# The first stage of a two-layer decoder step: queue order, the place of the first weights, and the loads of the tap rows

## The chip, the cores and the metric

One Trainium2 chip, one core of it, one launch. The number is the device time of one execution in microseconds (us), lower is better. TensorE, VectorE, ScalarE, GpSimd and SyncE are called PE, DVE, ACT, POOL and SP, as in the profile; "PEld" is PE's load of the stationary operand.

## The reference, cut to what matters

A prompt of 512 tokens and a sample of 8 sequences with 4 tokens each go through two layers of width 1024 in fp32. The part that this change touches is the beginning of layer 0:

```
m = silu(c) @ ada_w[0, 0] + ada_b[0, 0]          # c: 1 + 8 rows; shift, scale, gate
h = x * (1 + scale) + shift                      # the modulation
a, g = split(h @ conv_pw1_w + conv_pw1_b)        # 1024 -> 2048
u = a * sigmoid(g)
y = depthwise convolution of u over 31 tokens, then a norm, silu and a product with conv_pw2_w
```

After it come a residual and norm, an MLP of width 4096, layer 1 with stick-breaking attention over a paged cache of 2048 tokens for each sample, and a second MLP.

## The kernel before, in words

The prompt lies transposed in SBUF, eight tiles of 128 features by 512 tokens. A product in near-fp32 is made of three fp32r matmuls (`mm3`, lines 310 to 315: high weight by high x, low by high, high by low), so each weight tile is split by ACT (the rounded copy, `wsplit`, line 304) and DVE (the rest, line 305), and each h tile likewise (lines 329 and 330). The Tile framework writes all semaphores and, with a simulated timeline, the order of each engine's instructions; a `NoSync` edge (`order`, line 317) or `tc.issue_after` fixes the order of two instructions on one engine. An instruction's place in an engine's queue is thus not its place in the text, but each engine runs its queue in order.

The first stage in the text:

- c, constants and the first four blocks of `ada_w` (`ada_load`, line 189, 1 MB each, two transfers, SP's queue) are loaded; the second four follow when the ring of four buffers has room. The parameter rows `prow` go over ACT's queue (lines 201 to 208), x over POOL's (line 216).
- x is transposed by PE into PSUM and copied back by DVE (lines 586 to 595).
- The modulation is made in two halves `h` of 512 columns of shift and of scale: four blocks each with products into one PSUM tile (line 606), a copy by ACT (line 609), a turn to feature-major (`to_fm`, line 548), and the bias (lines 636 to 638). Half 0 gives h tiles 0 to 3, half 1 tiles 4 to 7 (lines 640 and 641).
- Four chunks c of `conv_pw1_w` (loop at line 738) are staged by `wstage` on ACT's queue, two loads of 1 MB for a chunk, three buffers. Each chunk serves the sample (line 747) and the prompt. Chunk 0 holds four weight tiles split ahead and runs k outermost over four PSUM accumulators:

```
            for k in range(KT):
                for a, (whi, wlo) in zip(accs, ws):
                    mm3(a, whi[:, k, :], wlo[:, k, :], hhi[k], hlo[k], k == 0, k == KT - 1)
```

- `axd` (lines 647 to 650) is x times a constant, spilled to DRAM by POOL's queue for the residual much later. `ud` holds the prompt's u in DRAM with zero padding, written at lines 629 and 630, from which the convolution is read again (line 683).
- Two feature tiles of the convolution are done by DVE with 30 steps each (line 670), the other six by PE (line 693).
- The attention's head biases are loaded by 20 small DMAs on POOL's queue (lines 818 and 824), with the page table and a broadcast of the biases (828, 830).

From there two generators, one for the sample and one for the prompt, are merged by written costs into one stream.

Of the kernel before, what the change touches and what calls it, by code (L numbers as in the profile page):

```python
# [8 lines left out]
F32 = mybir.dt.float32  # L9
# [10 lines left out]
KT = 8  # L20
# [48 lines left out]
C1_W = 128 + 32 + 64 + 32  # L69
# [3 lines left out]
def shape_consts():  # L73
# [11 lines left out]
    c1 = np.concatenate([ident, sel4, sel2, nmask, causal], 1)  # L85
# [25 lines left out]
def yoco_step_kernel(  # L111
# [64 lines left out]
    nmask = c1[:, 224:256]  # L176
    ones32 = base.tile([P, 32], F32, name="ones32")
# [10 lines left out]

    def ada_load(n):
        blk = ring("adaw")  # L190
        h, kk = divmod(n, 4)
        for kp in range(2):
            r = kk * 256 + kp * P
            dma(blk.rearrange("p (k o c) -> p k o c", k=2, o=2)[:, kp],
                ada_w[0, 0, r : r + P, 0 : 2 * D].rearrange("p (o f) -> p o f", o=2)[:, :, h * 512 : h * 512 + 512])
        first_blk.append(blk)
# [11 lines left out]
    nc.scalar.dma_start(prow[25:56, 0:D], conv_dw_w[0])  # L208
# [86 lines left out]
    def wstage(src, k):  # L295
        st = wp.tile([P, 2048], F32, tag="stage", bufs=STB, name="stage")
        nc.scalar.dma_start(st.rearrange("p (k c) -> p k c", k=k), src.rearrange("(k p) c -> p k c", p=P))
        return st.rearrange("p (k c) -> p k c", k=k)

    def wsplit(st, c0, cw, wp=wp):  # L300
# [3 lines left out]
        nc.scalar.copy(hi, st[:, :, c0 : c0 + cw])  # L304
        vec.tensor_tensor(lo, st[:, :, c0 : c0 + cw], hi.bitcast(F32), op=ALU.subtract)  # L305
        return hi, lo
# [280 lines left out]
    for hf in range(2):  # L587
        pts = []
        for kk in range(4):
            pts.append((pm if kk < 3 else aux)("xT"))  # L590
            for i in range(4):
                tr(pts[kk][:, i * P : i * P + P], xn[2 * i + hf][:, kk * P : kk * P + P], ident)
        for kk in range(4):
            ubuf[4 * hf + kk] = xn[2 * kk + hf]
            vec.tensor_copy(xn[2 * kk + hf], pts[kk])
    a00 = base.tile([P, KT, 9], F32, name="a00")
    b00 = base.tile([P, KT, 9], F32, name="b00")
    ada_sb = []
    for h in range(2):
        acc = aux("ada_A00")  # L600
        for kk in range(4):
            if h:
                ada_load(4 + kk)
            blk = first_blk[4 * h + kk]
            for g in range(4):
                mm(acc[32 * g : 32 * g + 32, :], cT[:, 2 * kk + g // 2, :], blk[:, g * 512 : g * 512 + 512],
                   start=(kk == 0), stop=(kk == 3), tile_position=(0, 32 * g))
        sb = stmp([P, 512], "ada0", tag="s512")
        last_act = nc.scalar.copy(sb, acc)
        ada_sb.append(sb)  # L610

    pt = aux("pt_p")
    for k in range(KT):
        tr(pt[:, k * 64 : k * 64 + NR], prow[0:NR, k * P : k * P + P], ident[0:NR, 0:NR])
    vec.tensor_copy(prm.rearrange("p r k -> p k r"), pt.rearrange("p (k r) -> p k r", k=KT)[:, :, 0:NR])
    vec.tensor_scalar_mul(aln, prm[:, R_LNG : R_LNG + 8, :], ALPHA)

    spt = aux("xsT")
    for k in range(KT):
        tr(spt[:, k * 32 : k * 32 + 32], xs_row[:, k * P : k * P + P], ident[0:32, 0:32])  # L620
    xsT = sfm("xsT", "sv", 2)
    vec.tensor_copy(xsT, spt[:, 0:256].rearrange("p (k t) -> p k t", k=KT))
# [4 lines left out]
    vec.memset(utail, 0.0)  # L627
    ud = dr.tile([KT, P, T + 32], F32, name="ud")
    pdma(ud[:, :, 0 : CW - 1].rearrange("k p t -> p k t"), utail[:, :, 0 : CW - 1])
    pdma(ud[:, :, T + CW - 1 :].rearrange("k p t -> p k t"), utail[:, :, 0:2])  # L630
    hhi, hlo = xtiles()
    for k in range(KT):
        if k % 4 == 0:
            us = to_fm(ada_sb[k // 4], "adat_A00")
            for t, o in ((b00, 0), (a00, 1)):
                vec.tensor_tensor(t[:, k : k + 4, :], us[:, 4 * o : 4 * o + 4, 0:9],
                                  prm[:, o, k : k + 4].unsqueeze(2).to_broadcast([P, 4, 9]), op=ALU.add)
            vec.tensor_scalar_add(a00[:, k : k + 4, :], a00[:, k : k + 4, :], 1.0)
        h = tmp("h")
        act(h, ubuf[k], AF.Identity, scale=a00[:, k, 8:9], bias=b00[:, k, 8:9])  # L640
        split(h, hhi[k], hlo[k])
    s_h = sfm("hT0", "hT", 2)
    vec.tensor_tensor(s4(s_h), s4(xsT), smod(a00), op=ALU.mult)
    vec.tensor_tensor(s4(s_h), s4(s_h), smod(b00), op=ALU.add)
    s_ax = sfm("sax", "sax")
    vec.tensor_scalar_mul(s_ax, xsT, ALPHA)
    for k in range(KT):
        t = tmp("ax0")
        nc.scalar.mul(t, ubuf[k], ALPHA)
        pdma(axd[0][k], t)  # L650

# [86 lines left out]
    for c in range(4):  # L738
        with tc.issue_after((first_act if c == 0 else last_act).ins):
            st = [wstage(conv_pw1_w[0, :, o * D + c * 256 : o * D + c * 256 + 256], KT) for o in range(2)]  # L740
# [16 lines left out]
        for i in range(2):  # L757
# [5 lines left out]
            vec.tensor_copy(sfull[:, kt, :, CW - 1 : CW + 3], su[:, kt, :].rearrange("p (s q) -> p s q", q=NQ))  # L763
        accs = []
        if c == 1:
            state_in()
            sconv(0)
        if c:
            sconv(c)
        if c == 0:  # L770
            p1c = ExitStack()
            plc = pool(p1c, "p1c", "right")
            ws = [wsplit(st[o], i * P, P, plc if i else wp) for i in range(2) for o in range(2)]
            accs = [pm("pw1") for _ in range(3)] + [aux("pw1")]
            for k in range(KT):
                for a, (whi, wlo) in zip(accs, ws):
                    mm3(a, whi[:, k, :], wlo[:, k, :], hhi[k], hlo[k], k == 0, k == KT - 1)
            p1c.close()
# [8 lines left out]
        for i in range(2):  # L787
# [21 lines left out]
            if kt not in TAPS:  # L809
                pdma(ud[kt][:, CW - 1 : T + CW - 1], u)  # L810
# [4 lines left out]

    bq = base.tile([P, 8], F32, name="bq")
    for g in range(4):
        pdma(bq[32 * g : 32 * g + 32, 0:4],
            attn_bias[0].rearrange("(q g) -> g q", g=4)[g : g + 1, :].to_broadcast([32, 4]))
        for hh in range(2):  # L820
            r = 32 * g + 16 * hh
            for u in range(2):
                hd = u * 8 + hh * 4 + g
                pdma(bq[r : r + 16, 4 + u : 5 + u], attn_bias[0:1, hd : hd + 1].to_broadcast([16, 1]))
    nbq = base.tile([P, 2], F32, name="nbq")
    nc.gpsimd.tensor_scalar_mul(nbq, bq[:, 4:6], -1.0)
    ptab = base.tile([P, NS, NPG], I32, name="ptab")
    pdma(ptab.rearrange("p s g -> p (s g)"), page_table.rearrange("(o s) g -> o (s g)", o=1).to_broadcast([P, NS * NPG]))
    bias_p = base.tile([P, 2 * H], F32, name="bias_p")
    pdma(bias_p[:, 0:H], attn_bias.to_broadcast([P, H]))  # L830
    nc.gpsimd.tensor_scalar_mul(bias_p[:, H:], bias_p[:, 0:H], -1.0)
# [640 lines left out]
```

## Time and profile before

| | us |
|---|---|
| median of 3 runs (lowest to highest) | 1671.01 (1669.94 to 1671.44) |
| the profiled execution | 1672.76 |
| its span, first to last instruction | 1671.0 |
| PE busy in it | 1564.6 (94%) |
| DVE busy | 956.5 (57%) |
| ACT busy | 568.6 (34%) |
| POOL busy | 188.4 (11%) |

The busy share is a mean over stages. Whether a shorter first stage makes the whole shorter depends on what the first stage waits for and on whether the engines behind it are full or wait for something that does not move with it.

### The profile page before, as it was taken

The page shows a single profiled execution, that of the slowest core. Times are in us where ns is not written, and L with a number is a line of the kernel's source. Part 1 is how long each engine was busy: PE and PEld are TensorE (multiplying, and loading weights), DVE is VectorE, ACT ScalarE, POOL GpSimd, SP SyncE. Part 2 cuts the span into 40 slices and gives each one's busy share as a digit, 9 for nine tenths or more (in the row PEclk, how much of TensorE's full clock was granted, in tenths as well). Part 3 has the DMA queues.
Part 4 walks back from the last instruction along what each step waited for, and adds up shares of the span by engine and source line. Part 5 has one row for each costly group of instructions (what it writes and reads, how often), then busy time and mean ns, then how long its engine had stood idle before and what let it go on. Part 6 is the DMA issues. An engine that isn't in the chain of part 4 may idle for free.

```text
span 1671.0 us, 25460 instructions
## 1 busy us (share of the span) xinstructions
PE 1564.6 (94%) x10489; PEld 1090.3 (65%) x10489; DVE 956.5 (57%) x1812; ACT 568.6 (34%) x903; POOL 188.4 (11%) x221
## 2 busy tenths in 40 slices
PE   4899988989999999999899999889889999999995
PEld 2566424656777777777468775546777767556885
DVE  2399637385576755655643457975774533332546
ACT  1322105153332332323332444852272323223332
POOL 4100110000112111110012112021101000000002
PEclk9899999989999999999999999999999999999998
DMA  8787879878676866576879878355546585995221
GB/s 292 247 294 265 265 230 393 318 261 309 235 267 243 322 227 234 218 279 227 318 271 316 296 239 325 134 213 185 192 162 244 184 312 180 356 346 191 85 70 51
DMA packets 152968, 409.25 MB, mean 245 GB/s; under 512 B 8807, under 2 KB 82823, under 8 KB 128261
## 3 DMA queue, kind: packets, MB, share of 16 engines
q1 hardware_dynamic: 48739, 159.76, 25.7%
q0 software_dynamic: 23584, 149.07, 24.7%
q10 hardware_dynamic: 80530, 98.80, 17.8%
q8 instruction: 82, 1.34, 0.3%
q14 instruction: 33, 0.27, 0.0%
HBM read 390.57 MB, written 17.88 MB: 244 GB/s over the span
## 4 chain that ended last, share of the span: by engine, by line
PE 73%; issue 10%; DVE 8%; DMA 6%; ACT 1%; POOL 1%; SPq 0%; DVEq 0%; ACTq 0%; POOLq 0%
PE pd L311 17%; PE pd L315 17%; PE pd L314 17%; PE zt L1001 3%; PE av L1052 3%; PE sd_acc L535 2%; PE cv L693 2%; DMA stage<-in_conv_pw_w_dram 2%; PE w_acc L562 1%; DVE v L670 1%; PE ada_A L237 1%; PE lnT L350 1%; DMA kraw<-in_cache_k_dram,krow 1%; PE pw L311 1%; PE pw L314 1%
## 5 line engine op out<-in xcount | busy, mean ns | idle before, releaser
L305 DVE TENSOR_TENSOR wlo<-stage,whi 128x1024 fp32r<-128x1024 f32 x184 | 223.3, 1217 | 252.2 <-ACT whi L304 251.8
L304 ACT CAST whi<-stage 128x1024 fp32r<-128x1024 f32 x184 | 191.6, 1046 | 423.1 <-PE pd L315 353.1
L311 PE MATMUL pd<-xhi,whi 128*128 128x512 f32 (+1 forms) x832 | 321.0, 387 | 11.3 <-ACT whi L304 5.5
L314 PE MATMUL pd<-xhi,wlo 128*128 128x512 f32 (+1 forms) x832 | 318.9, 384 | 2.1 <-DVE wlo L305 2.0
L315 PE MATMUL pd<-xlo,whi 128*128 128x512 f32 (+1 forms) x832 | 313.0, 387 | 5.5 <-DVE xlo L444 5.0
L995 DVE STREAM_TRANSPOSE kt<-kraw 128x512 f32<-128x512 f32 x256 | 164.3, 685 | 123.7 <-DMA kraw<-in_cache_k_dram,krow 84.0
L311 PE MATMUL pd<-h2h,whi 128*128 128x512 f32 (+1 forms) x544 | 206.7, 388 | 1.6 <-DVE v L1170 1.0
L315 PE MATMUL pd<-h2l,whi 128*128 128x512 f32 (+1 forms) x544 | 205.2, 383 | 0.0
L314 PE MATMUL pd<-h2h,wlo 128*128 128x512 f32 (+1 forms) x544 | 204.9, 381 | 0.0
L311 PEld LDWEIGHTS pd<-xhi,whi 128*128 128x128 f32 x832 | 161.1, 194 | 60.9 <-issue 14.3
L315 PEld LDWEIGHTS pd<-xlo,whi 128*128 128x128 f32 x832 | 157.0, 193 | 58.4 <-issue 15.4
L314 PEld LDWEIGHTS pd<-xhi,wlo 128*128 128x128 f32 x832 | 161.0, 193 | 42.8 <-issue 12.7
L1170 DVE SCALAR_TENSOR_TENSOR v<-pd,mod_B,v 128x512 f32<-128x512 f32 x120 | 87.8, 745 | 115.8 <-PE pd L315 115.4
L973 POOL DMA_INDIRECT kraw<-in_cache_k_dram,krow x64 | 65.9, 1029 | 631.1 <-DVE kt L995 396.0
L311 PEld LDWEIGHTS pd<-h2h,whi 128*128 128x128 f32 x544 | 101.9, 188 | 34.6 <-issue 10.4
L1145 ACT ACTIVATE relu<-pd 128x512 f32<-128x512 f32 (+1 forms) x68 | 38.9, 572 | 240.3 <-PE pd L315 235.1
L315 PEld LDWEIGHTS pd<-h2l,whi 128*128 128x128 f32 x544 | 101.8, 188 | 28.6 <-issue 9.4
L314 PEld LDWEIGHTS pd<-h2h,wlo 128*128 128x128 f32 x544 | 102.2, 188 | 25.2 <-issue 6.7
L973 POOL DMA_INDIRECT vt<-in_cache_v_dram,vrow x64 | 67.0, 1047 | 273.7 <-PE av L1052 235.3
L1001 PE MATMUL zt<-kt,qb 128*32 128x128 f32 x2048 | 77.0, 280 | 5.2 <-DVE kt L995 5.2
L1001 PEld LDWEIGHTS zt<-kt,qb 128*32 128x32 f32 x2048 | 53.4, 111 | 30.3 <-issue 14.7
L352 DVE BATCH_NORM_STATS2 bn<-lnT 128x6 f32<-128x128 f32 x160 | 36.5, 285 | 62.4 <-PE lnT L350 62.2
(299 smaller groups left out, 2014.6 us busy)
## 6 DMA issues: line engine op xcount, KB each, us to landing
sw<-in_mlp_w_dram SPq DMA_DIRECT2D x64, 1024.0 KB
stage<-in_mlp_w_dram ACTq DMA_DIRECT2D x64, 1024.0 KB
adaw<-in_ada_w_dram SPq DMA_DIRECT2D x40, 1024.0 KB
stage<-in_conv_pw_w_dram ACTq DMA_DIRECT2D x12, 1024.0 KB
adaw<-in_ada_w_dram SPq DMA_DIRECT2D x16, 512.0 KB
swkv<-in_w_kv_dram SPq DMA_DIRECT2D x8, 1024.0 KB
stage<-in_w_kv_dram ACTq DMA_DIRECT2D x8, 1024.0 KB
ur<-ud POOLq DMA_DIRECT2D x24, 270.0 KB, 7.5
```

Of the source, the lines that this page charges most:

```text
L304: nc.scalar.copy(hi, st[:, :, c0 : c0 + cw])
L305: vec.tensor_tensor(lo, st[:, :, c0 : c0 + cw], hi.bitcast(F32), op=ALU.subtract)
L311: first = mm(out, whi, xh, start=start, stop=False)
L314: mm(out, wlo, xh, start=False, stop=False)
L315: latest[:] = [mm(out, whi, xl, start=False, stop=stop)]
L352: vec.bn_stats(self.st[:, i, k, :], pt[:, i * P : i * P + P])
L973: nc.gpsimd.indirect_dma_start(out=out, out_offset=None, in_=cache.rearrange("g (r e) h d -> (g r) (e h d)", e=2), in_offset=bass.Indirect ...
L995: ins = vec.transpose(kt[:, 2 * x : 2 * x + 2, :], raw[x].rearrange("p (e c) -> p e c", e=2)[:, :, c0 : c0 + 256])
L1001: behind(mm(zt[u][32 * g : 32 * g + 32, f * P : f * P + P], qb[:, u, hh * 8 + bl].rearrange("p x q -> p (x q)"), kt[:, :, bl * 32 : bl * 3 ...
L1052: behind(mm(av[32 * g : 32 * g + 32, :], wT[u][:, i, e, a, :], vt[:, e * D + u * 512 : e * D + u * 512 + 512], start=(a == 0 and i == 0), ...
L1145: latest_act[:] = [act(r, a, AF.Relu)]
L1170: ins = vec.scalar_tensor_tensor(v[kt][:, ts], a, gt[:, kt, 8:9], v[kt][:, ts], op0=ALU.mult, op1=ALU.add)
```

## The change

- The modulation's first half is finished alone. The order on PE is written out: all transposes of x, blocks 0 to 2, the transposes of the parameter rows and of the sample's x (`params`), block 3. Its ACT copy (`half_act`) comes ahead of every weight cast.
- The two stage loads of chunk 0 go to SP's queue, behind the transfers of blocks 0 to 3, and blocks 4 to 7 behind them.
- Chunk 0's products come in three groups: accumulators 0 and 2 (both from the first stage load) for k 0 to 3; accumulators 1 and 3 for k 0 to 3, with blocks 4 to 7 between; all four for k 4 to 7 after the second half.
- DVE's order of weight rests, h casts and h rests is written out (`first_chain`). The second four copies of x out of PSUM go to ACT.
- The bias and the "1 +" of the modulation become one DVE instruction each.
- The sample's h, the `axd` spill and the sample's products with chunk 0 stand behind chunk 0's products in the text.
- The zero padding of `ud` comes from a tile of its own, set by POOL behind the last `axd` transfer.
- The 20 small bias DMAs go. One broadcast of the biases is loaded behind the last u, and 13 small DVE instructions build `bq` and `nbq` from it. The page table is loaded there too.
- The rows of the convolution's taps in `prow` are loaded as 16 and 15 rows instead of 31.

```diff
     def ada_load(n):
...
+            if n >= 4:
+                order(ins, sp_chain[-1])
+        sp_chain.append(ins)
...
-    nc.scalar.dma_start(prow[25:56, 0:D], conv_dw_w[0])
+    nc.scalar.dma_start(prow[25:41, 0:D], conv_dw_w[0, 0:16])
+    nc.scalar.dma_start(prow[41:56, 0:D], conv_dw_w[0, 16:31])
...
+    def wsplit(st, c0, cw, wp=wp, after=None, chain=None):
...
+        ins = nc.scalar.copy(hi, st[:, :, c0 : c0 + cw])
+        if after:
+            order(ins, after)
+        ins = vec.tensor_tensor(lo, st[:, :, c0 : c0 + cw], hi.bitcast(F32), op=ALU.subtract)
+        if chain is not None:
+            in_turn(chain, ins)
...
+            if hf:
+                x_in = nc.scalar.copy(xn[2 * kk + hf], pts[kk])
+            else:
+                vec.tensor_copy(xn[2 * kk + hf], pts[kk])
...
+    def ada_mms(n, after):
+        if n >= 4:
+            ada_load(n)
+        kk = n % 4
+        for g in range(4):
+            ins = order(mm(ada_acc[-1][32 * g : 32 * g + 32, :], cT[:, 2 * kk + g // 2, :], first_blk[n][:, g * 512 : g * 512 + 512],
+                           start=(kk == 0), stop=(kk == 3), tile_position=(0, 32 * g)), after)
+        return ins
+
+    def ada_fin(h):
+        sb = stmp([P, 512], "ada0", tag="s512")
+        done_act = nc.scalar.copy(sb, ada_acc[-1])
+        us = to_fm(sb, "adat_A00")
+        for t, o in ((b00, 0), (a00, 1)):
+            vec.scalar_tensor_tensor(t[:, 4 * h : 4 * h + 4, :], us[:, 4 * o : 4 * o + 4, 0:9], float(o),
+                                     prm[:, o, 4 * h : 4 * h + 4].unsqueeze(2).to_broadcast([P, 4, 9]), op0=ALU.add, op1=ALU.add)
+        return done_act
...
+    for n in range(4):
+        last_tr = ada_mms(n, last_tr)
+        if n == 2:
+            last_tr = params(last_tr)
+    half_act = ada_fin(0)
...
+            if c:
+                with tc.issue_after(last_act.ins):
+                    st.append(wstage(src, KT))
+            else:
+                st.append(wstage(src, KT, nc.sync, sp_chain))
...
+            weights(0, 0, half_act)
+            h_act = first_h(0)
+            weights(1, 0, half_act)
+            for k in range(1, 4):
+                h_act = first_h(k)
+            for i in range(2):
+                weights(i, 1, h_act)
+            for k in range(4):
+                products(k, (0, 2))
+            ada_acc.append(aux("ada_A00"))
+            ada_mms(4, latest[0])
+            for k in range(4):
+                products(k, (1, 3))
+                if k % 2:
+                    ada_mms(5 + k // 2, latest[0])
+            ada_mms(7, latest[0])
+            last_act = ada_fin(1)
+            for k in range(4, KT):
+                first_h(k)
+            for k in range(4, KT):
+                products(k, range(4))
+            p1c.close()
...
+            sample_pw1(0, st)
...
+            if kt == 0:
+                pad = order(nc.gpsimd.memset(zpad, 0.0), axd_dma)
+                pdma(ud[:, :, 0 : CW - 1].rearrange("k p t -> p k t"), zpad[:, :, 0 : CW - 1])
+                pdma(ud[:, :, T + CW - 1 :].rearrange("k p t -> p k t"), zpad[:, :, 0:2])
```

## Rows read from the trace of the kernel before

**Rows 1.** Stretches of the start: engine busy us (and instructions), granted clock, DMA share, GB/s.

```profile
16.00:20.00 4.00, 0.37 (x2) 0.19 (x4) 0.00 (x0) 0.00 (x0) 2.39 (x4) 1.00 1.08 358
...
40.00:44.00 4.00, 0.06 (x1) 0.00 (x0) 0.70 (x1) 1.78 (x2) 0.00 (x0) 0.74 0.26 63
...
48.00:52.00 4.00, 4.00 (x16) 1.15 (x15) 2.28 (x9) 2.65 (x4) 0.00 (x0) 0.50 0.64 144
52.00:56.00 4.00, 4.00 (x17) 2.20 (x16) 2.27 (x5) 0.28 (x1) 0.00 (x0) 0.98 0.68 223
```

The columns are the stretch, its length, then busy time (and number of instructions) of PE, PEld, DVE, ACT and POOL, the granted clock, the DMA share and GB/s.

**Rows 2.** The stretch behind the first stage, same columns.

```profile
83.00:180.00 97.00, 94.97 (x570) 64.90 (x569) 96.46 (x170) 24.38 (x42) 7.16 (x13) 1.00 0.85 293
```

**Rows 3.** Who waited for whom until 60 us: total us, times, longest.

```profile
ACT whi L304 <- DMA stage<-in_conv_pw_w_dram: 30.2, 2, 23.5
...
PEld ada_A L606 <- DMA adaw<-in_ada_w_dram: 14.0, 5, 5.5
```

**Rows 4.** Instructions in order of time, until 60 us: start, us, engine, what.

```profile
13.97 1.94 PE L606 MATMUL ada_A<-adaw,cT 128*32 128x512 f32 x8
...
34.89 1.05 PE L606 MATMUL ada_A<-adaw,cT 128*32 128x512 f32 x4 [0.59 <-DMA adaw<-in_ada_w_dram]
...
42.22 1.99 ACT L304 CAST whi<-stage 128x1024 fp32r<-128x1024 f32 x2 [6.74 <-DMA stage<-in_conv_pw_w_dram]
43.30 2.36 DVE L305 TENSOR_TENSOR wlo<-stage,whi 128x1024 fp32r<-128x1024 f32 x2 [3.98 <-ACT whi L304]
44.12 0.58 ACT L609 COPY ada<-ada_A 128x512 f32<-128x512 f32 x1
...
48.80 0.20 DVE L636 TENSOR_TENSOR b<-adat_A,prm 128x36 f32<-128x36 f32 x1 [0.77 <-PE adat_A L548]
...
52.23 0.50 PE L311 MATMUL pw<-xhi,whi 128*128 128x512 f32 x1
```

**Rows 5.** The same view, PE alone, from 64 to 100 us.

```profile
64.27 1.00 PE L548 MATMUL adat_A<-c,ada 128*128 128x64 f32 x8
66.88 1.93 PE L747 MATMUL pw1s<-stage,hT 128*32 128x256 f32 x32 [1.61 <-DVE hT L644]
...
73.74 0.97 PE L755 MATMUL us<-c,pw1sb 128*128 128x32 f32 x8
...
78.12 0.40 PE L311 MATMUL pw<-xhi,whi 128*128 128x512 f32 x1
...
83.49 0.39 PE L315 MATMUL pw<-xlo,whi 128*128 128x512 f32 x1
...
99.32 1.07 PE L237 MATMUL ada_B<-adaw,cT 128*32 128x512 f32 x8
```

**Rows 6.** DMA until 60 us: rate in 40 slices of 1.5 us; issues with size, us to landing.

```profile
GB/s 0 195 344 171 363 391 386 369 365 329 363 363 366 329 217 279 288 252 262 380 246 268 377 361 345 380 114 36 51 287 363 53 156 175 71 467 76 309 145 330
...
adaw<-in_ada_w_dram SPq DMA_DIRECT2D x16, 512.0 KB
v<-in_x_prompt_dram POOLq DMA_DIRECT2D x8, 256.0 KB, 7.5
...
ud<-utail POOLq DMA_DIRECT2D x1, 120.0 KB, 7.7
```

**Rows 7.** Instructions by line: ns (least, median, most), first and last start in us.

```profile
L640 ACT ACTIVATE h<-v,b,a x8: 797/801/813, 49.4 to 68.0; 128x512 f32<-128x512 f32 x8
...
L329 DVE CAST xhi<-h x8: 420/425/429, 50.2 to 69.7; 128x512 fp32r<-128x512 f32 x8
L330 DVE TENSOR_TENSOR xlo<-h,xhi x8: 685/689/693, 50.7 to 70.2; 128x512 fp32r<-128x512 f32 x8
...
L824 POOL DMA_DIRECT2D bq<-in_attn_bias_dram x16: 484/488/518, 9.1 to 29.3; - x16
```

**Rows 8.** ACT in order of time: a stage load issued, and a cast that waited for it.

```profile
104.85 0.37 ACTq L297 DMA_DIRECT2D stage<-in_conv_pw_w_dram  x1
...
116.47 1.05 ACT L304 CAST whi<-stage 128x1024 fp32r<-128x1024 f32 x1 [1.30 <-DMA stage<-in_conv_pw_w_dram]
```

**Rows 9.** The chain of waits: the first PE convolution (start, us, what).

```profile
174.38 0.99 PE cv L693 x8
```

More of the change, by code (lines that the diff above doesn't have):

```diff
@@ L612, in yoco_step_kernel, with params @@
[L612 to L622, printed above, removed]
+    def params(after):
+        pt = aux("pt_p")
+        for k in range(KT):
+            order(tr(pt[:, k * 64 : k * 64 + NR], prow[0:NR, k * P : k * P + P], ident[0:NR, 0:NR]), after)
+        vec.tensor_copy(prm.rearrange("p r k -> p k r"), pt.rearrange("p (k r) -> p k r", k=KT)[:, :, 0:NR])
+        vec.tensor_scalar_mul(aln, prm[:, R_LNG : R_LNG + 8, :], ALPHA)
+        spt = aux("xsT")
+        for k in range(KT):
+            last = order(tr(spt[:, k * 32 : k * 32 + 32], xs_row[:, k * P : k * P + P], ident[0:32, 0:32]), after)
+        vec.tensor_copy(xsT, spt[:, 0:256].rearrange("p (k t) -> p k t", k=KT))
+        return last
@@ L626, in yoco_step_kernel @@
     utail = pl.tile([P, KT, CW + 1], F32, name="utail")
-    vec.memset(utail, 0.0)
+    zpad = pl.tile([P, KT, CW + 1], F32, name="zpad")
     ud = dr.tile([KT, P, T + 32], F32, name="ud")
[L629 to L650, printed above, removed]
     s1 = ExitStack()
@@ L737, in yoco_step_kernel, with sample_pw1 @@
     early = itertools.chain(ada_b_(0), ada_a(0, 1), *[(ada_b_(1), ada_a(1, 1), ada_a(1, 0))[i] for i in range(EARLY)])
-    for c in range(4):
-        with tc.issue_after((first_act if c == 0 else last_act).ins):
-            st = [wstage(conv_pw1_w[0, :, o * D + c * 256 : o * D + c * 256 + 256], KT) for o in range(2)]
+    def sample_pw1(c, st):
         sps = []
@@ L763, in yoco_step_kernel @@
             vec.tensor_copy(sfull[:, kt, :, CW - 1 : CW + 3], su[:, kt, :].rearrange("p (s q) -> p s q", q=NQ))
+    for c in range(4):
+        st = []
+        for o in range(2):
+            src = conv_pw1_w[0, :, o * D + c * 256 : o * D + c * 256 + 256]
+            if c:
[3 more added lines that the diff above has]
+                st.append(wstage(src, KT, nc.sync, sp_chain))
         accs = []
+        if c:
+            sample_pw1(c, st)
         if c == 1:
@@ L772, in yoco_step_kernel, with weights, products @@
             plc = pool(p1c, "p1c", "right")
-            ws = [wsplit(st[o], i * P, P, plc if i else wp) for i in range(2) for o in range(2)]
             accs = [pm("pw1") for _ in range(3)] + [aux("pw1")]
+            ws = [None] * 4
+            def weights(i, o, after):
+                ws[2 * i + o] = wsplit(st[o], i * P, P, plc if i else wp, after, first_chain)
+            def products(k, which):
+                for j in which:
+                    mm3(accs[j], ws[j][0][:, k, :], ws[j][1][:, k, :], hhi[k], hlo[k], k == 0, k == KT - 1, *latest)
+            weights(0, 0, half_act)
[20 more added lines that the diff above has]
+            p1c.close()
+            s_h = sfm("hT0", "hT", 2)
+            vec.tensor_tensor(s4(s_h), s4(xsT), smod(a00), op=ALU.mult)
+            vec.tensor_tensor(s4(s_h), s4(s_h), smod(b00), op=ALU.add)
+            s_ax = sfm("sax", "sax")
+            vec.tensor_scalar_mul(s_ax, xsT, ALPHA)
             for k in range(KT):
-                for a, (whi, wlo) in zip(accs, ws):
-                    mm3(a, whi[:, k, :], wlo[:, k, :], hhi[k], hlo[k], k == 0, k == KT - 1)
-            p1c.close()
+                t = tmp("ax0")
+                nc.scalar.mul(t, ubuf[k], ALPHA)
+                axd_dma = pdma(axd[0][k], t)
+            sample_pw1(0, st)
             pld = pool(p1, "p1d", "left")
```

73 lines of the change are left out of this document (36 added, 37 removed).

## The prediction

> **What bounds the kernel now.** I read the page first (PE is busy for 94% of the span, so a gain must come from PE's idle time), then the stretches of the start, then who waited for whom there, and then the instructions one by one. From 83 to 180 us PE is busy for 94.97 of 97 us and DVE for 96.46 [rows 2]; the PE time that can be won lies ahead of that, and the first 52 us hold it: PE is nearly empty from 16 to 20 us and from 40 to 44 us [rows 1]. The first product of the convolution's projection starts at 52.23 us, the last of chunk 0 at 83.49 us [rows 4, 5].
>
> Two things hold that start back. The transfers compete: the stage loads are wanted by ACT's casts, which wait 30.2 us for them, while the modulation's products wait 14.0 us for their blocks [rows 3]. So the first half's last block is multiplied only at 34.89 us, and the second stage load lets its cast start only at 42.22 us [rows 4]. And ACT's queue is in the wrong order: the copy of the finished first half (line 609) stands behind the casts of the second stage load and runs at 44.12 us, 8.2 us after its products ended at 35.94 us [rows 4]. PE then runs out of work and its granted clock falls to the lower of its two levels: 0.50 of 2.4 GHz from 48 to 52 us, 0.98 from 52 us on [rows 1].
>
> **The change part by part.** All against the profiled execution (span 1671.0 us, 1672.76 us as timed, 1.75 us above the median of 1671.01).
>
> *Transfers.* Ahead of the first half's end there are now 8 transfers of 512 KB and 8 of 256 KB for x [rows 6], and about 0.5 MB of small ones: 6.8 MB. The first 15 slices of 1.5 us moved 6.83 MB in the kernel before [rows 6], so this is landed by 22.5 us. The slices from 4.5 us to 21 us (leaving the ramp aside) run near 365 GB/s and those from 21 to 28.5 us near 260; the slow ones lie beside the small bias transfers (16 of the 20 are issued between 9.1 and 29.3 us [rows 7]) and the padding, which are gone from here, and I take 365: 2.9 us for 1 MB. In one queue the stage loads land at 25.4 and 28.3 us, blocks 4 to 7 at 31.1, 34.0, 36.9 and 39.8 us. At 260 GB/s they would end at 46.7 us instead.
>
> *First half.* Block 3's products by the slower of their rows 1.94 us (eight at 13.97 us [rows 4]): 22.5 + 1.9 = 24.4 us. PE now has all x transposes and the parameters' transposes ahead of it; x is among the 6.8 MB, and PE had room (0.37 of 4 us busy from 16 us [rows 1]), so I cost that order at nothing. If x came last it would cost what x is late. ACT's copy 0.58, the turn 1.00 at full clock [rows 5] and up to 2.0 at half of it, of which I take 2.0, two small DVE operations at 0.20 (the third is gone) and 0.1 for handing over, h 0.80, its cast 0.43 [rows 4, 7]: 4.3 us, 28.7 us, and with 0.3 us for the other handoffs 29.0 us for the first product instead of 52.23. The first stage load (25.4 us) and its cast and rest (1.0 + 1.2 us [rows 4]) are ready by 27.6 us.
>
> *Products, k 0 to 3.* 24 products start between 78.12 and 83.49 us, 0.2335 us each [rows 5]. The first 24: PE needs 5.6 us; DVE needs one h rest, one weight rest and three tiles at 0.43 + 0.69 us [rows 7], 5.2 us, and six products follow the last: DVE sets the end at 35.6 us. Then four blocks at 1.07 us (the row of eight at full clock, 99.32 us [rows 5]) and 24 products: 4.3 + 5.6 = 9.9 us, to 45.5 us. Block 7 is needed at 44.4 us, and is there at 39.8.
>
> *Second half.* Copy 0.58, turn 1.00, DVE 0.5 with its handoff, h 0.80, cast 0.43 [rows 4, 5, 7]: 3.3 us, to 48.8 us. Then 48 products, 11.2 us, and the sample's 1.93 + 0.97 us [rows 5], which the kernel before had done inside this stage: 62.9 us. There the same work ends at 83.8 us. Raw gain 20.9 us.
>
> *What I take off.* (1) The `axd` spill depends only on x, and ACT has room for it between 34 and 45 us: 2 MB of writes on POOL's queue beside blocks 4 to 7, 5.8 us at 365 GB/s, so block 7 could land at 45.6 us instead of being needed at 44.4; between 0 and 3 us, I take 1.5. The Trainium skill (DMA: Bandwidth & Descriptors, Queues, rings and completion order) says that each DMA engine goes round the queues that have work, a packet at a time. By that rule the spill takes its full share from the blocks, and the gain is smaller by the upper end; the rows fit it, since both stage loads crept beside SP's blocks [rows 3]. (2) The gap on PE from 24.4 to 29.0 us is like the one from 40 us on, after which the clock was at its lower level. If the first 24 products all ran there they would take twice 5.6 us, 4.5 us past what DVE allows; if none, nothing. I take 2, because in the kernel before the products from 52.23 us on came 0.235 us apart at once. (3) The sample's products with chunk 0 now stand behind the prompt's, and they keep the stage buffers that chunk 1's second load needs: between 0 and 8 us (see the rivals); in the kernel before the sample's products slipped into the wait for the second half's h [rows 5], and can again, so I take 1. (4) The 13 small DVE operations for the biases, at 0.20 us like the nearest small one [rows 4] 2.6 us, come after the last u and are read only by the attention: 0 if DVE has room there, 2.6 if PE waits for them; I take 0.4. The four copies of x on ACT fall where ACT has nothing else: 0. The padding takes 7.7 us to land [rows 6] at about 70 us, and its reader, the first PE convolution, ran at 174.38 us [rows 9]: 0, and 7.7 if that cover were gone. The tap rows' split and the page table's move: 0, since only the parameters' transposes and the attention read them.
>
> *What is behind it.* Both PE and DVE are full from 83 to 180 us, and both queues start at the end of chunk 0's products, so the whole stretch moves with it. DMA could stop this: in that stretch it moves 293 GB/s [rows 2], 28.4 MB, which at 365 GB/s needs 78 of 97 us. There is room, and the loads start when ring buffers come free, which is earlier by about as much.
>
> Sum: 20.9 - 1.5 - 2 - 1 - 0.4 = 16.0 us. 1671.0 - 16.0 = 1655.0 us.
>
> **The rivals.**
>
> *Half of it.* Chunk 1's second weight load comes late. There are three stage buffers; it needs one of chunk 0's. If PE takes the sample's products only behind the prompt's, it is issued at 63 us, and such a load took up to 11.6 us from issue to the cast that waited for it [rows 8]: 74.5 us, split at 76.7 us. PE has 24 products of chunk 1, 5.6 us, to 68.5 us, and waits about 8 us: gain 8, 1663 us. For it: the new place in the text. Against it: the order follows simulated time, and there the wait for the second half's h is open to them. The same size results if the transfers do not come sooner as worked out: with the first half still done at 35.9 us and only ACT's wrong order mended, 1671 - 8.2 = 1663 us.
>
> *Nothing.* The stretch from 83 us does not move, because its length is set by transfers (0.85 share [rows 2]) or because the order of the merged streams shifts for the worse by as much: 1669 to 1673 us. Against it: PE's own 94.97 us there.
>
> *Slower: the clock.* The order written out makes PE wait at three places instead of one, with little work between. From 29.0 us to the end it has 22.4 us of products, 4.3 of blocks, 1.0 of turn and 2.9 for the sample, 30.6 us at full clock. At 1.2 GHz throughout they take 61.2 us, with the two waits (29.0 us before, 2.3 us of the second half) to 92.5 us, 8.7 us later than 83.8: 1679.7 us. It turns into a loss once more than 22 of the 30.6 us run at the lower level. For it: the clock was at 0.50 from 48 to 52 us, after PE had been nearly empty from 40 to 44 us [rows 1]. Against it: it was back at 0.98 as soon as products ran.
>
> **How the numbers follow.** The forecast (gain 10 to 22) has 0.66, half of it (4 to 10) 0.19, nothing 0.08, slower 0.07. About 0.2%, 3.3 us, is what a measurement of this kernel can tell from no change. Faster by more: 0.66 + 0.19 = 0.85; within: 0.08; slower: 0.07. The time is the forecast's, 1655.0 us. The range leaves out the losses and the largest gains: the low end is the raw gain with 2 us for bounds that turned out at nothing or better, 1671 - 23 = 1648; the high end takes in the half, 1671 - 5 = 1666.
>
> **What would show it.** In the trace after: ACT's copy of the first half near 25 us and the first product near 29 us; stage casts that no longer wait until 42 us; block 7 multiplied by 46 us; the last product of chunk 0 near 61 to 66 us; DVE full from then on; and the first PE convolution at about 158 us instead of 174. If the first half is not done before 30 us the transfers were not mended. If chunk 0 ends in time but PE idles afterwards for a stage load, it is the first rival; a granted clock of 0.50 beyond 35 us is the third. The forecast is wrong outright if chunk 0 ends by 66 us and the time still lies above 1667 us.

## The result and the profile after

The changed kernel takes 1651.21 us (median of 4 runs, 1650.56 to 1653.03) against 1670.79 us (1669.94 to 1671.44) beside it: a ratio of 0.9881 with a 95% interval of 0.9867 to 0.9894, 19.6 us less. Forecast were 1655.0 us and 16.0 us of gain. The profiled execution took 1650.69 us with a span of 1648.9 us.

The stretches of the start, as in [rows 1] (stretch, its length, busy time and count of PE, PEld, DVE, ACT and POOL, granted clock, DMA share, GB/s):

```profile
16.00:20.00 4.00, 4.00 (x21) 2.63 (x24) 1.15 (x2) 1.60 (x4) 0.00 (x0) 1.00 1.05 388
...
28.00:32.00 4.00, 1.67 (x4) 1.12 (x4) 3.08 (x6) 3.45 (x6) 0.00 (x0) 0.76 1.05 381
32.00:36.00 4.00, 4.00 (x15) 3.15 (x15) 3.90 (x8) 1.82 (x2) 0.00 (x0) 0.82 1.05 388
36.00:40.00 4.00, 4.00 (x22) 2.36 (x21) 1.60 (x2) 0.00 (x0) 0.00 (x0) 1.00 0.94 304
...
48.00:52.00 4.00, 2.38 (x21) 1.69 (x25) 2.52 (x7) 2.41 (x5) 0.00 (x0) 0.82 0.86 311
52.00:56.00 4.00, 4.00 (x32) 2.43 (x25) 2.89 (x6) 2.36 (x5) 1.06 (x2) 0.76 1.03 397
```

PE, nearly empty from 16 to 20 us before, is full there. Its two gaps are short (26.3 to 30.3 us, and 47.5 to 50.7 us with only a turn in it), and behind each the granted clock is below 1. The means of 0.76 and 0.82 hide two shorter spells at the lower level, of some 3.4 us each; taken alone they read (same columns):

```profile
30.10:33.40 3.30, 3.07 (x7) 2.14 (x8) 3.23 (x6) 3.30 (x5) 0.00 (x0) 0.50 1.05 387
...
50.60:53.90 3.30, 3.18 (x32) 1.61 (x32) 3.20 (x7) 2.86 (x5) 0.41 (x1) 0.50 1.02 401
```

The waits until 60 us answer to [rows 3] (engine, line, waited for, total us, times, longest):

```profile
ACT L226 <- DMA prow<-in_conv_dw_b_dram: 9.5, 1, 9.5
...
DVE wlo L319 <- ACT whi L316: 2.5, 1, 2.5
...
ACT whi L316 <- DMA stage<-in_conv_pw_w_dram: 1.3, 1, 1.3
```

ACT's 30.2 us of waiting for stage loads are 1.3 us, and the products' 14.0 us for blocks are no longer among the waits of 1 us and more. New is the first row: the sigmoid of c waits until the last `prow` load is issued on ACT's queue.

The instructions that answer to [rows 4, 5], in order of time (start, us, engine, what):

```profile
23.31 1.23 PE L638 MATMUL ada_A<-adaw,cT 128*32 128x512 f32 x8
...
24.58 0.58 ACT L644 COPY ada<-ada_A 128x512 f32<-128x512 f32 x1 [4.13 <-PE ada_A L638]
...
26.46 1.99 ACT L316 CAST whi<-stage 128x1024 fp32r<-128x1024 f32 x2 [1.29 <-DMA stage<-in_conv_pw_w_dram]
27.54 1.23 DVE L319 TENSOR_TENSOR wlo<-stage,whi 128x1024 fp32r<-128x1024 f32 x1 [2.48 <-ACT whi L316]
28.68 0.19 DVE L647 SCALAR_TENSOR_TENSOR b<-adat_A,prm 128x36 f32<-128x36 f32 x1
...
30.33 0.79 PE L327 MATMUL pw<-xhi,whi 128*128 128x512 f32 x1 [4.01 <-DVE xhi L656]
...
37.62 1.06 PE L638 MATMUL ada_A<-adaw,cT 128*32 128x512 f32 x8
...
45.59 1.92 PE L638 MATMUL ada_A<-adaw,cT 128*32 128x512 f32 x16
...
47.58 0.58 ACT L644 COPY ada<-ada_A 128x512 f32<-128x512 f32 x1 [13.76 <-PE ada_A L638]
...
50.72 3.50 PE L765 MATMUL pw1s<-stage,hT 128*32 128x256 f32 x32 [1.40 <-DVE hT L838]
...
65.34 0.97 PE L773 MATMUL us<-c,pw1sb 128*128 128x32 f32 x8
```

The first half's copy runs 19.5 us earlier than before, and chunk 0's last product ends at 65.3 us instead of 83.8. The stretch that follows is nearly as full as in [rows 2] (PE 93.54 of 97 us against 94.97, DVE 94.58 against 96.46):

```profile
66.00:163.00 97.00, 93.54 (x557) 63.78 (x557) 94.58 (x170) 25.28 (x46) 11.44 (x20) 1.00 0.89 303
```

The DMA rates until 60 us, in 40 slices of 1.5 us as in [rows 6]:

```profile
GB/s 0 185 359 167 302 386 389 303 366 275 378 388 388 385 378 351 350 348 359 378 386 386 386 391 384 340 105 262 5 153 459 35 284 279 398 408 400 335 346 401
```

Where the slices from 21 to 28.5 us ran near 260 GB/s before, they now run at 348 to 378.

Two more places give the whole account. First and last start of the convolution's products (the row after answers to [rows 9]) and of the attention's mask products, of the changed kernel (the columns: ns least, median, most, then first and last start in us, shapes):

```profile
L713 PE MATMUL cv<-ur,wk x384: 589/592/1061, 158.5 to 230.1; 128*32 128x512 f32 x192
...
L1397 PE MATMUL pz<-maskx,maskw x128: 216/216/284, 996.1 to 1110.0; 64*128 64x128 bf16 x128
```

and of the kernel before:

```profile
L693 PE MATMUL cv<-ur,wk x384: 589/592/1061, 174.3 to 247.4; 128*32 128x512 f32 x192
...
L1327 PE MATMUL pz<-maskx,maskw x128: 212/216/311, 1011.6 to 1132.0; 64*128 64x128 bf16 x128
```

The convolution starts 15.8 us earlier and the attention 15.5. The attention's last mask product is 22.0 us earlier, and so is the end (span 1671.0 to 1648.9). The attention's stretch itself became shorter, 113.9 us instead of 120.4, though no line of the attention was changed.

### The profile page after: what moved, and what is told of

Read it like the earlier page. It is cut to its first block, busy times and chain, and to the rows that moved or that the text cites. A ratio compares the mean times of both kernels' runs of the same rounds, so it can differ in the third digit from the quotient of the medians.

```text
span 1648.9 us, 25461 instructions
## 1 busy us (share of the span) xinstructions
PE 1553.3 (94%) x10489; PEld 1088.2 (66%) x10489; DVE 954.8 (58%) x1818; ACT 569.4 (35%) x907; POOL 181.2 (11%) x201
## 3 DMA queue, kind: packets, MB, share of 16 engines
q1 hardware_dynamic: 50819, 161.86, 26.3%
## 4 chain that ended last, share of the span: by engine, by line
PE 78%; DMA 8%; issue 6%; DVE 5%; ACT 2%; POOL 1%; DVEq 0%; SPq 0%; POOLq 0%; ACTq 0%
PE pd L327 18%; PE pd L331 18%; PE pd L330 17%; PE zt L1071 3%; PE av L1122 3%; PE sd_acc L551 3%; PE cv L713 2%; DMA adaw<-in_ada_w_dram 2%; PE w_acc L578 1%; DMA kraw<-in_cache_k_dram,krow 1%; PE pw L327 1%; PE pw L330 1%; PE pw L331 1%; DMA stage<-in_conv_pw_w_dram 1%; PE ada_A L246 1%
## 5 line engine op out<-in xcount | busy, mean ns | idle before, releaser
L327 PEld LDWEIGHTS pd<-xhi,whi 128*128 128x128 f32 x832 | 160.7, 193 | 59.7 <-issue 13.7
L1240 DVE SCALAR_TENSOR_TENSOR v<-pd,mod_B,v 128x512 f32<-128x512 f32 x120 | 87.8, 745 | 114.1 <-PE pd L331 113.9
L327 PEld LDWEIGHTS pd<-h2h,whi 128*128 128x128 f32 x544 | 101.9, 188 | 34.8 <-issue 10.4
L1043 POOL DMA_INDIRECT vt<-in_cache_v_dram,vrow x64 | 70.3, 1098 | 273.4 <-PE av L1122 222.9
```

Of the source, the lines that this page charges most:

```text
L327: first = mm(out, whi, xh, start=start, stop=False)
L1043: nc.gpsimd.indirect_dma_start(out=out, out_offset=None, in_=cache.rearrange("g (r e) h d -> (g r) (e h d)", e=2), in_offset=bass.Indirect ...
L1240: ins = vec.scalar_tensor_tensor(v[kt][:, ts], a, gt[:, kt, 8:9], v[kt][:, ts], op0=ALU.mult, op1=ALU.add)
```

## The experiments

All ratios are to the kernel before, run beside the kernel on the same chip (its medians: 1670.79 us beside the changed kernel, 1669.62 beside e1 to e4, 1669.27 beside e5 to e7, 1671.24 beside e8 and e9). "First product" is the first of chunk 0; "stretch" is from the first to the last mask product of the attention.

| kernel | us | ratio, interval | first product | first convolution | stretch |
|---|---|---|---|---|---|
| before, profiled | 1672.76 | 1 | 52.23 | 174.3 | 120.4 |
| rb, before again | 1669.85 | 1 | 49.89 | 172.0 | 118.3 |
| after | 1651.21 | 0.9881 (0.9867 to 0.9894) | 30.33 | 158.5 | 113.9 |
| e1 | 1665.54 | 0.9971 (0.9959 to 0.9982) | 50.35 | 173.5 | 114.2 |
| e2 | 1655.45 | 0.9919 (0.9905 to 0.9933) | 33.34 | 160.4 | 113.4 |
| e3 | 1652.10 | 0.9901 (0.9885 to 0.9917) | 33.45 | 164.6 | 113.2 |
| e4 | 1660.34 | 0.9952 (0.9936 to 0.9967) | 49.34 | 170.2 | 113.0 |
| e5 | 1655.34 | 0.9921 (0.9901 to 0.9940) | 34.91 | 162.4 | 113.4 |
| e6 | 1650.35 | 0.9887 (0.9871 to 0.9904) | 29.30 | 166.8 | 113.6 |
| e7 | 1657.05 | 0.9922 (0.9906 to 0.9938) | 33.83 | 165.5 | 113.0 |
| e8 | 1659.07 | 0.9928 (0.9914 to 0.9941) | 29.17 | 160.7 | 113.1 |
| e9 | 1663.94 | 0.9952 (0.9939 to 0.9966) | 30.29 | 163.1 | 112.6 |

The first convolution is a weak mark by itself: e6 has it 8.3 us later than the changed kernel and takes the same time.

**e1, ACT's order alone**, on the kernel before (`after` is the copy of the first half):

```diff
-        nc.scalar.copy(hi, st[:, :, c0 : c0 + cw])
+        ins = nc.scalar.copy(hi, st[:, :, c0 : c0 + cw])
+        if after:
+            order(ins, after)
```

> The kernel before with one edit: the four weight casts of chunk 0 stand behind ACT's copy of the modulation's first half. If ACT's order was a large part of the first stage's loss: the copy runs near 36.5 us instead of 44.1 us; but the second stage load still lands at 42 us and DVE's queue still has its weight rests ahead of the bias, so the first product comes near 47 us instead of 52.2 us, 4 to 5 us of gain in the first stage. PE's queue in the attention is here nearly the one of the changed kernel (3 differences against it, 33 against the kernel before). If that order is what made the attention stretch 6 us shorter, the time is 1660 to 1663 us; if the attention stretch was only a spread between executions, it is 1666 to 1667 us. If ACT's order cost nothing and the attention is a spread, 1671 us.

ACT and DVE of e1, in order of time:

```profile
36.16 0.59 ACT L611 COPY ada<-ada_A 128x512 f32<-128x512 f32 x1 [26.18 <-PE ada_A L608]
...
41.97 2.94 ACT L304 CAST whi<-stage 128x1024 fp32r<-128x1024 f32 x3 [4.28 <-DMA stage<-in_conv_pw_w_dram]
43.05 2.36 DVE L307 TENSOR_TENSOR wlo<-stage,whi 128x1024 fp32r<-128x1024 f32 x2 [4.10 <-ACT whi L304]
45.32 0.96 DVE L619 COPY prm<-pt_p 128x448 f32<-128x448 f32 x1
...
48.41 0.19 DVE L640 TENSOR_TENSOR b<-adat_A,prm 128x36 f32<-128x36 f32 x1
...
50.35 0.79 PE L313 MATMUL pw<-xhi,whi 128*128 128x512 f32 x1 [3.63 <-DVE xhi L331]
```

The copy came 8 us earlier, and the first product only 1.9 us earlier than in the profile before. It is not earlier than in rb. DVE's queue holds the same mistake: the weight rest at 43.05 us waits for a cast that waits for the stage load, and the parameters' copy and the bias stand behind it. The convolution starts at 173.5 us, between the two executions of before. e1's 4.8 us (0.0029 of 1670) lie in the attention's stretch.

**rb, the kernel before, profiled again**, for the stretch of the attention.

> The kernel before, unchanged, profiled once more, to tell order from spread in the attention stretch. If the order of PE's queue there makes it long, first to last mask product takes 119 to 122 us again (five kernels with the changed order took 113.0 to 114.2). If it was a spread between executions, it can come out at 114 us here.

118.3 us: long again, so the difference is not the spread of one execution. By the names of their tiles, PE's instructions come in that stretch in one order in the changed kernel and in e1 to e9 (but for one or two records missing in some traces), and in another in the two executions of before, which have 32 more products `zt<-kt,qb` in it (320 against 288). The ten kernels with the one order have 112.6 to 114.2 us, the two executions of the other 120.4 and 118.3. The rows of before, of rb and of e1 (one execution each):

```profile
1011.60:1132.00 120.40, 102.02 (x1097) 62.29 (x1097) 104.32 (x186) 77.43 (x150) 20.34 (x20) 0.93 0.59 213
```

```profile
1008.70:1127.00 118.30, 99.03 (x1096) 60.61 (x1097) 103.03 (x183) 77.37 (x150) 19.37 (x19) 0.96 0.59 217
```

```profile
1011.50:1125.70 114.20, 96.20 (x1066) 58.66 (x1065) 104.07 (x186) 76.79 (x150) 20.92 (x19) 0.97 0.59 216
```

DVE has the same work in each (103 to 104 us). PE is idle for as long (18 to 19 us), but busy for 3 to 6 us longer in the long stretch, with 30 more instructions in it. Part of that is the granted clock (0.93 and 0.96 against 0.97), but the clock alone does not make the stretch long: e4 and e9 have 0.95 there, in stretches of 113.0 and 112.6 us. The instructions were not only moved: from the first `kv_acc` product to the stretch it is 604.9 us before and 605.4 after (starts at 406.7 and 390.7 us), and from its end to that of the span 539.0 and 538.9. So the 4.4 to 6.5 us are won. The order of the merged streams follows simulated time; a small shift at the start tips it 1000 us later. Which part of the order matters was not tried.

**e2, the stage loads back on ACT's queue**, PE's and DVE's order as in the changed kernel:

```diff
-                st.append(wstage(src, KT, nc.sync, sp_chain))
+                with tc.issue_after(first_act.ins):
+                    st.append(wstage(src, KT))
```

> The changed kernel with chunk 0's two stage loads back on ACT's queue, beside the blocks; PE's and DVE's queues hold the same instructions in the same order as in the changed kernel. If the transfers' competition is the larger half: block 3's products near 33 to 35 us instead of 23 to 24 us, first product near 39 us instead of 30.3 us, chunk 0's end 7 to 9 us later, time 1658 to 1660 us. If only ACT's order mattered: first half still done near 24 us or the delay taken up later, time at most 1653 us.

```profile
27.89 1.05 PE L638 MATMUL ada_A<-adaw,cT 128*32 128x512 f32 x4 [0.99 <-DMA adaw<-in_ada_w_dram]
28.98 0.59 ACT L644 COPY ada<-ada_A 128x512 f32<-128x512 f32 x1 [8.59 <-PE ada_A L638]
...
33.34 0.79 PE L327 MATMUL pw<-xhi,whi 128*128 128x512 f32 x1 [2.62 <-DVE xhi L656]
```

These are PE and ACT of e2 in order of time. Block 3 ends 4.4 us later than in the changed kernel (28.94 against 24.54 us), the first product is 3.0 us later, the attention starts 3.0 us later (999.1 against 996.1), the time is 4 us longer by the medians and 6 by the ratios, whose intervals are apart. So the queue, not only the written order, brings that part: the two loads no longer share the engines with the blocks that are wanted first. The Trainium skill (DMA: Bandwidth & Descriptors, Queues, rings and completion order) has the engines go round the queues that have work. By that rule 2 MB in another queue can push block 3 back by up to their own time, an estimated 5.4 us at 385 GB/s, and the 4.4 us agree with it.

**e3, the 20 small bias loads back at the start** of the changed kernel (its 13 DVE instructions go; the old loads, with the page table and the broadcast of the biases, stand behind chunk 3's loop in the text and are issued early, as before).

> The changed kernel with the 20 small bias loads and the page table back on POOL's queue at the start (the padding stays late). If the small transfers slow the start as I took it (260 instead of 365 GB/s for some 7 us): first half done 1 to 3 us later, 1652 to 1654 us. If they cost nothing: 1651 us, first product at 30.3 us.

The DMA rates of e3 until 60 us, and its packets:

```profile
GB/s 0 191 329 191 339 384 393 320 321 283 341 382 345 381 362 60 312 342 261 379 370 339 392 388 388 388 369 209 45 113 218 19 180 412 85 289 328 412 406 382
DMA packets 9336, 17.47 MB, mean 291 GB/s; under 512 B 1246, under 2 KB 3878, under 8 KB 9318
```

One slice falls to 60 GB/s (22.5 to 24 us) and the next three lie at 261 to 342. From 22.6 to 23.4 us nothing moves at all (DMA share 0.00), so what is lost there is not the small loads' own share of the engines; what stopped the transfers was not found. There are 631 more packets under 512 B than in the changed kernel (615), at most 0.3 MB, and yet the first stage cast runs at 29.59 us instead of 26.46 and the first product 3.1 us later. Of that delay 0.0020 of the time is left, 3 us, and the two intervals overlap: beside the rest of the change the bias part is worth 0 to 7 us.

**e4, the bias part alone** on the kernel before: one broadcast behind the last u and 13 DVE instructions in place of the 20 loads, the page table with it.

> The kernel before with the bias part alone (one broadcast behind the last u, 13 small DVE instructions). The first stage keeps ACT's order and the shared queues, so its gain is 0 to 2 us (fewer small transfers). PE's queue in the attention stretch is here exactly that of the changed kernel. If that order makes the stretch short, first to last mask product there takes 114 us instead of 120 us and the time is 1664 to 1666 us; if the 6 us were a spread or came from the earlier first stage, the stretch takes 120 us and the time is 1669 to 1671 us.

1660.34 us, below both: 8 us. The first convolution is at 170.2 us against 172.0 and 174.3, the last at 238.3 against 244.9 and 247.4, and the attention's stretch is the short one (113.0). So 2 to 4 us come at the start, some 5 within the convolution, where PE's longest wait for u read back is 2.2 us instead of 5.4, and 5 to 7 in the attention. That is more than 8, partly because the profiled execution (1657.87 us) lies 2.5 us below e4's median. The DMA rates of e4 until 60 us:

```profile
GB/s 0 208 321 179 322 399 385 366 386 365 293 305 309 311 374 379 369 348 376 392 387 385 374 365 140 36 36 210 356 163 61 262 46 210 374 344 199 180 254 295
```

From 21 to 28.5 us they lie at 348 to 379, where the kernel before has 217 to 288 [rows 6]. What I had called nothing or 0.4 us of loss is the part of the change with most of its effect elsewhere.

**e5, the tap rows in one load of 31** in the changed kernel:

```diff
-    nc.scalar.dma_start(prow[25:41, 0:D], conv_dw_w[0, 0:16])
-    nc.scalar.dma_start(prow[41:56, 0:D], conv_dw_w[0, 16:31])
+    nc.scalar.dma_start(prow[25:56, 0:D], conv_dw_w[0])
```

> The changed kernel with the 31 tap rows in one load again; PE's and DVE's queues are the same. If the split is needed: the parameters' transposes, now ahead of block 3, wait for the rows, PE waits there 2 to 10 us and the time is 1653 to 1660 us. Rival: the split only puts a tenth load ahead of ACT's sigmoid, which ran at 10.8 us instead of 9.0 us in the kernel before; without it the start is up to 1.9 us earlier and the time is 1649 to 1651 us.

SP's queue and PE of e5, where the changed kernel has the first block's products at 18.93 us and the stage loads' issue at 18.02 us with 1.56 us:

```profile
19.14 1.11 PE L607 MATMUL xT<-c,v 128*128 128x128 f32 x4 [0.95 <-DMA v<-in_x_prompt_dram]
20.18 3.78 PE L637 MATMUL ada_A<-adaw,cT 128*32 128x512 f32 x16
```

```profile
20.01 4.43 SPq L305 DMA_DIRECT2D stage<-in_conv_pw_w_dram  x2
```

The sigmoid ran 1.7 us earlier (9.09 against 10.80), since one load less stands ahead of it, but x came later and every block after it: 8.83 MB had landed by 30 us against 9.65. The copy is at 29.38 us, 4.8 us later, and the time 4 us longer by the medians and 7 by the ratios, whose intervals are apart. I had set the split at 0. The copy's 4.8 us are the size to explain. The Trainium skill (DMA: Bandwidth & Descriptors, Why a DMA increments its semaphore by 16 and not by 1) lets a transfer use as many of the 16 engines as the largest divisor, up to 16, of its number of rows. By that rule 16 rows go to 16 engines and 15 to 15, but 31 rows to one; 124 KB there, at a sixteenth of 385 GB/s, take an estimated 5.3 us, and each block needs that engine too. The trace agrees on the one engine: on ACT's queue the 31 packets of 4 KB start one after another from 11.40 to 21.63 us, no two at the same time, where the changed kernel's 16 all start within 0.5 us and its 15 within 0.4. They took 10.4 us, twice the estimate; that the blocks waited for that engine was not read, so for the 4.8 us the cause is argued and not shown. The kernel before and e4 have the same load of 31 rows, and e4's slices from 10.5 to 24 us all lie at 293 or more, so it does not cost the same everywhere.

**e6, bias first and the second gap filled** in the changed kernel (`bias_op` is the bias of the first half on DVE, now ahead of the first weight rest):

```diff
+            first_chain.append(bias_op[0])
...
-            weights(1, 0, half_act)
+            weights(1, 0, h_act)
...
-            for k in range(4):
-                products(k, (1, 3))
-                if k % 2:
-                    ada_mms(5 + k // 2, latest[0])
-            ada_mms(7, latest[0])
+            for k in range(2):
+                products(k, (1, 3))
+            for n in range(5, 8):
+                latest[:] = [ada_mms(n, latest[0])]
+            for k in range(2, 4):
+                products(k, (1, 3))
```

> The changed kernel with two orders altered: DVE's bias instructions of the first half stand ahead of the first weight rest (which had held them from 26.4 to 28.7 us), and blocks 5 to 7 stand ahead of the products of accumulators 1 and 3 for k 2 and 3, so that these 12 products lie in the wait for the second half. If both waits cost what the trace shows: first product near 29.2 us instead of 30.3 us, chunk 0 done 3 to 4 us earlier, time 1647 to 1649 us. If blocks 6 and 7 land too late for the earlier place, PE waits 1 to 3 us for them and the second edit gives nothing: 1650 us. If the stretch behind does not move, 1651 us.

Granted clock and work of e6 from 48 to 52 us, then its sample's products:

```profile
48.00:52.00 4.00, 3.08 (x37) 2.16 (x38) 3.84 (x9) 4.00 (x8) 0.30 (x1) 1.00 0.87 339
```

```profile
48.92 1.93 PE L767 MATMUL pw1s<-stage,hT 128*32 128x256 f32 x32 [1.40 <-DVE hT L842]
...
61.99 0.97 PE L775 MATMUL us<-c,pw1sb 128*128 128x32 f32 x8
62.89 1.07 PE L767 MATMUL pw1s<-stage,hT 128*32 128x256 f32 x16
65.61 1.07 PE L767 MATMUL pw1s<-stage,hT 128*32 128x256 f32 x16 [1.65 <-DMA stage<-in_conv_pw_w_dram]
68.13 1.92 PE L775 MATMUL us<-c,pw1sb 128*128 128x32 f32 x8 [1.46 <-ACT pw1sb L770]
```

With products in the gap the clock stays at 1.00, and the 32 products take 1.93 us instead of 3.50. Chunk 0 ends 3.4 us earlier. Then PE waits for chunk 1's second stage load, and the next `us` starts at 68.13 us, where the changed kernel has it at 68.11. Nothing is left of the 3.4 us: the time is the same. That is close to the first rival's mechanism, one step further on.

**e7, the written order without two of the edits on transfers**: e2 and e3 together. The tap rows' split and the late padding stay in.

> The changed kernel with the stage loads back on ACT's queue and the small bias loads back at the start: the written order of the first stage (and the attention order that comes with it) without the two edits on transfers. If the edits add up: 5 us for the queue and 3 us for the small loads over 1651 us, 1658 to 1660 us. If the written order hides the transfers, 1655 us as with the first of them alone. If the written order is worth nothing by itself, 1664 us (the attention's 6 us alone).

1657.05 us: 13.0 us of the gain without the queue and without the bias part, 5 to 7 of them in the attention. The tap rows' split, worth 4 to 7 us in e5, is still among the rest, so what the written order brings by itself in the first stage was not measured. Block 3 waits for its transfers as in e2 (copy at 29.46 us). e2's and e3's losses are 6 and 3 us by ratio, together 7; the intervals are too wide to tell this from a sum.

The DMA rates of e7 until 60 us:

```profile
GB/s 0 218 287 244 337 388 377 344 320 287 342 370 353 369 364 345 374 359 354 348 349 382 378 386 385 388 152 5 0 68 251 8 164 448 71 238 287 366 410 406
```

The small loads are issued here as in e3, from 8 to 25 us, and yet no slice from 21 to 28.5 us lies below 345. So they do not slow the transfers in every setting. What else it takes was not found; one execution of each was profiled.

**e8 and e9, the `axd` spill later**, in e6 and in the changed kernel: its loop moved to chunk 2, the padding ordered behind the first u.

```diff
+        if c == 2:
+            for k in range(KT):
+                t = tmp("ax0")
+                nc.scalar.mul(t, ubuf[k], ALPHA)
+                axd_dma = pdma(axd[0][k], t)
...
-            if kt == 0:
-                pad = order(nc.gpsimd.memset(zpad, 0.0), axd_dma)
+            if kt == 1:
+                pad = order(nc.gpsimd.memset(zpad, 0.0), u_dma)
```

> This is e6 (bias first on DVE, the gap filled by blocks 5 to 7) with the axd spill moved in the text from chunk 0 to behind chunk 1's sample work, and the padding ordered behind the first u transfer instead of the last axd transfer. e6 ended chunk 0 3.4 us earlier than the changed kernel (61.99 against 65.34 us) but its time was the same. Theory: the transfers took the gain: chunk 1's second stage load is issued at 51.13 us on ACT's queue, its issue takes 6.91 us, and its cast runs only at 65.55 us after waiting 3.06 us for it, beside 2 MB of axd writes. Without them the load lands some 4 us sooner, chunk 1's first product of the prompt starts by 69 us instead of 71.99, and the time is 1646.5 to 1648.5 us. Rival A, the load's own issue is what is late (it waits for a stage buffer or for a place in the queue): cast still near 65 us, time 1649 to 1651.5. Rival B, DVE is full from 75 us and sets the rest: first product near 69 us, yet the first PE convolution still at 165 to 167 us, time 1649 to 1651.5.

> The changed kernel with the same move of the axd spill (and of the padding's place) and nothing else. There chunk 0 ends later (65.34 us) and chunk 1's stage cast waited only 0.42 us for its load, so the theory that the load binds only once chunk 0 is shorter expects no gain: 1649.5 to 1652 us. If the spill costs in the changed kernel too, by its writes beside the loads from 53 to 69 us, 1647 to 1649.

ACT and the waits of e8, ACT's and PE's:

```profile
61.83 1.05 ACT L316 CAST whi<-stage 128x1024 fp32r<-128x1024 f32 x1
```

```profile
ACT whi L316 <- DMA stage<-in_conv_pw_w_dram: 10.0, 2, 7.8
```

```profile
PE cv L715 <- DMA ur<-ud: 8.8, 2, 4.8
PE pw L327 <- ACT sg L871: 6.7, 1, 6.7
```

and PE's waits of e9:

```profile
PE cv L713 <- DMA ur<-ud: 10.9, 2, 5.5
PE pw L327 <- ACT sg L867: 6.2, 1, 6.2
```

The first row confirms the theory for its place: chunk 1's second cast runs at 61.83 us without a wait, 3.7 us earlier than in e6, and PE starts chunk 1's prompt products at 64.75 us instead of 71.99. The others (46 to 180 us, and PE from 60 to 260 us) show why the time is 7 us longer than e6's by the ratios all the same: the spill now lies beside the later stage loads, whose casts wait 10.0 us (1.0 in the changed kernel), and PE waits 6.7 us for ACT and 8.8 us for u read back (3.8 in e6). e9 is 12 us longer than the changed kernel by the ratios, and its PE waits the same way: 10.9 us for u read back, where the changed kernel has 5.0, and 6.2 for ACT, where it has none. Both totals went against every expectation. The spill has to lie somewhere, and where the changed kernel has it it costs less than in the other place tried.

## Why the prediction was right, step by step

- *Transfers, first half.* Forecast 24.4 us for the last products of block 3; measured 24.54. The rate taken, 365 GB/s instead of 260, is what the slices show (348 to 378). The stretch it was read from has one slice of 171 in it, at 4.5 us; from 6 us on its mean is 362. The reason given, the small loads, is borne out by e4 and e3 but not by e7. That the times agree to 0.1 us is in part luck: PE, whose new order the sum cost at nothing, was full from 16 to 24 us, and block 3's products began at 23.31 us right behind its transposes, without a wait for the block, and took 1.23 us instead of 1.94.
- *First product.* 29.0 us forecast, 30.33 measured. The turn was done at 26.3 us, 0.7 ahead of the sum's 27.0, which had taken 2.0 us for it instead of 1.10. But the bias waited on DVE behind the first weight rest until 28.68 us; my sum had the weight ready by 27.6 us and did not put it ahead of the bias. e6 swaps them: 29.30 us.
- *The gap and the clock.* Allowance (2) was needed, 2 us, and at two places. The first six matmuls behind the first gap lasted 0.63 to 0.79 us instead of 0.39 (granted clock 0.50). That the clock is back "as soon as products ran" does not hold here: behind each gap the first 3 us of products ran at the lower level. After the second the sample's products took 3.50 instead of 1.93 us, which the forecast had set at full clock. Blocks 4 to 7 and the second group ended at 47.5 us, not 45.5, for the 1.3 us of the first product and the clock. The slower rival had the mechanism right, but two stretches of 3.4 us at 0.50 are far from its 22 us at half.
- *Allowances (1) and (3).* Not needed. The spill started at 52.6 us, behind the blocks, not beside them; the stage buffer cost one wait of 0.42 us.
- *End of chunk 0.* 62.9 us forecast without allowances, 67.4 with the 4.5 us of (1) to (3); measured 65.3, or 66.2 with the sample's last 0.97 us, which the forecast counts in. Here too there is luck, as misses offset each other: 1.3 us of the first product were not in the sum, and the 2.5 us of (1) and (3) were not needed.
- *What is behind it.* The stretch moved almost as a whole: first convolution 158.5 us, forecast 158. This is the forecast's 16 us, 13.5 to 15.8 by which execution of before one takes. The first `kv_acc` product, behind the convolution, says the same: 390.7 us, against 406.7 and 403.6 in the two executions of before, 12.9 to 16.0.
- *What was missed.* The other 4 to 6 us are the attention's order. I had a shift of the merged streams only as a loss, in the rival "nothing". e1, e4 and rb show that any change tried here brings it. So the gain, 3.6 us past the forecast's, would have stayed in the range with several us less from the first stage, and does not confirm the sum; the rows of the first stage do.
- *"ACT's wrong order mended only: 8.2 us."* Wrong: e1 gains at most 2 us at the start. The time of one engine's late instruction is not what its repair brings, because DVE held the same wait behind it.
- *The biases and the tap rows at 0 or -0.4.* Right as a loss that does not show, wrong as a size: 0 to 7 us (e3) and 4 to 7 us (e5) of gain. They were inside the 365 GB/s of the first step, which I took without pricing the edits that bring it.

## What to carry to other kernels

Put the transfers that are wanted first ahead of the others in one queue, and keep away from them a load that goes a row at a time, as the 31 rows of e5 did: a load in another queue takes its share from the one that is waited for (4.4 us in e2). When an instruction stands behind a wait on one engine's queue, look for the same wait on the next engine before pricing the repair. After a change ahead of a stretch that a planner orders, compare that stretch's own length as well, and that of the kernel before twice.

## What the hardware showed that was not expected

Beside some 630 more packets under 512 B (at most 0.3 MB) one slice of 1.5 us ran at 60 GB/s in e3, where near 380 is usual, and three more below 345; with the same packets e7 had no such slice, so the cause is open. One load of 31 rows of 4 KB in place of 16 and 15 went a packet at a time for 10.4 us and left 0.8 MB less landed by 30 us. After gaps of 3 to 4 us with little on PE the granted clock read 0.50 for some 3.4 us, with the first six matmuls at 0.63 to 0.79 us; with products in the second gap it stayed at 1.00 (e6).
